# A decoder layer's trunk, run stage by stage over three token blocks instead of block by block, with Strassen's products added up in three PSUM banks

## The chip, the cores and the metric

The kernel runs on one core of a Trainium2 chip. The core has five engines with a queue of instructions each: TensorE (PE in the profile; its weight loads are PEld), VectorE (DVE), ScalarE (ACT), GpSimd (POOL) and SyncE (SP), which here only starts transfers. [...] The metric is device time in microseconds (us) from the start of the program to its end; lower is better.

## What is computed

One inference step of a decoder layer for 2048 prompt tokens and 32 sample tokens (8 requests of 4), all in float32, width 1024. First come the input projection, a gated linear recurrence on half of the heads and dilated window attention on the other half. The change touches none of that. It touches the trunk that follows, whose core in the reference is:

```python
mix = jnp.concatenate([o_a.astype(dt), o_b.reshape(bsz, t_len, B_WIDTH).astype(dt)], axis=-1)
h = x + mix @ w_o
hn = rmsnorm(h, norm_ffn_g)
u = hn @ w_gate
full = jnp.concatenate([conv_buf.astype(dt), u], axis=1)
c = conv_b
for j in range(CONV_W):
    c = c + conv_w[j] * full[:, j:j + t_len]
h = h + (jax.nn.silu(c) * (hn @ w_up)) @ w_down
new_conv = full[:, t_len:]
gate = jax.nn.sigmoid(rmsnorm(h, norm_ple_g) @ w_ple_gate)
h = h + gate * (p_emb.astype(dt) @ w_ple_proj)
```

w_gate and w_up are 1024 x 2816, w_down is 2816 x 1024, w_o and w_ple_gate are 1024 x 1024, w_ple_proj is 256 x 1024; the convolution runs over three neighbouring tokens of the same request. A final norm gives y.

## The kernel before

Features lie on partitions and tokens along the row. The trunk takes the tokens in three blocks: 704, 704 and 672 wide, the last of them 640 prompt tokens and the 32 sample tokens.

A float32 product is made from three matmuls (`mm3`, lines 131 to 134): an operand is split into a rounded part (ScalarE's copy) and the rest (a subtraction), and high by high, high by low and low by high are added up in PSUM. A weight is loaded 128 x 512 at a time, and `split` (lines 925 to 929) lets ScalarE round it (line 927) and VectorE and GpSimd by turns subtract (line 928).

`trunk_phase` (line 897) is one token block from start to end:

- **Out projection** (lines 968 to 1108): loads of the mix, 8 x 2 x 8 products of three matmuls, addition of x (line 1103). While it runs, the Strassen operands are made from h and the gains alone (`operands`, lines 989 to 1007), with subtractions on VectorE and GpSimd; the norm's factor per token (`rb`) is multiplied in later.
- **FFN** (lines 1163 to 1192): features two tiles of 128 at a time, eleven such pairs. Gate and up are one Strassen call each. `quarters` (line 1011) loads four weight quarters, GpSimd makes their four sums and differences, and all seven are split. `strassen` (line 1030) runs seven products of 12 matmuls over half a block of tokens, each into a bank of its own, and then puts them together: one copy on ScalarE (line 1042) and seven additions on VectorE (lines 1043 to 1049). `conv` (line 1111) multiplies by `rb` (lines 1115 and 1133) beside the convolution proper and copies the two border columns on VectorE (lines 1113 and 1120). The down projection of a pair (line 1157) is 16 output tiles of 6 matmuls, one behind another, each added into h by VectorE (line 1142); it runs one pair later, between gate and up.
- **Embedding stage** (lines 1195 to 1291): norm, `w_ple_gate`, sigmoid, `w_ple_proj`, final norm, output.

The norms' sums of squares go through small matmuls: columns (`rstd_cols`, line 105), a few small VectorE instructions (lines 91 to 96), and rows again (`bcast_rows`, line 120).

The phases of two blocks are stepped by turns (lines 1402 to 1413), so that the loads and the first out projection of block b+1 are written between the last embedding pieces of block b. h and all operands of a block stay in SBUF throughout. Products, downs and the rest share six banks, the norms have two.

The order of the instructions on each engine is not the order of the code: a planner simulates the program, and each engine takes the ready instruction that stands earliest in the code. On the chip the order is fixed, and an engine waits at an instruction whose inputs are late. All of the trunk's transfers are issued on SP's queue, except copies of the caches from DRAM to DRAM, which ScalarE's queue issues behind chosen rounding copies (`copy_after`).

## Time and profile before

| | |
|---|---|
| median of three runs | 3204.1 us (3198.14 to 3208.56) |
| the profiled execution's own time | 3206.86 us |
| its span, first to last instruction | 3204.7 us |
| busy in the span: TensorE, VectorE, GpSimd, ScalarE | 95%, 78%, 46%, 38% |
| mean granted clock of TensorE | 0.974 |
| traffic, mean | 408.89 MB, 128 GB/s |

Matmuls overlap each other in the trace, so TensorE's busy time hides short gaps; counts of matmuls per stretch of time tell more. A line number is that of the instruction's line in the kernel, often in a helper. A group's row gives line, engine, operation, output and inputs with their shapes, count, then busy us, mean ns of one, and the idle time of its engine before it with what ended it.

### The profile page before, as it was taken

To read this page: it belongs to the slowest core of one execution; us is meant where nothing else is said; L and a number is where in the kernel's file an instruction comes from. 1 tells how busy PE (TensorE), PEld (TensorE's weight loads), DVE (VectorE), ACT (ScalarE), POOL (GpSimd) and SP (SyncE) were. 2 spreads that over 40 slices of the span, in tenths; PEclk is the share of its full clock that TensorE was granted. 3 is DMA by queue.
4 is the path that set the end of the run, shared out by engine and by line. 5 is a ranking of instruction groups with operands and counts; after the bars stand their busy time and mean duration, and the time that the engine had idled before them with its cause. 6 is when DMAs were issued, how large, how long until landed. Compare 5 with 4: busy or idle time off the path is not lost.

```text
span 3204.7 us, 52298 instructions
## 1 busy us (share of the span) xinstructions
PE 3036.5 (95%) x19035; PEld 2795.5 (87%) x19035; DVE 2487.8 (78%) x4808; ACT 1226.7 (38%) x2441; POOL 1488.1 (46%) x1097
## 2 busy tenths in 40 slices
PE   8999999999889997899999999999999989999998
PEld 8988899977666666899999999999999988999998
DVE  6514588676788865888998758899998579999996
ACT  4112322221466653433334425333334244333343
POOL 1201122221454416656566458466564575655654
PEclk9999999999889998999999999999999999999999
DMA  5324333332456985343334242334433323433432
GB/s 181 105 102 145 93 113 115 121 126 82 118 135 191 266 278 162 105 130 113 119 126 140 80 136 68 129 126 136 134 117 105 99 94 128 136 124 106 130 109 79
DMA packets 241313, 408.89 MB, mean 128 GB/s; under 512 B 36832, under 2 KB 104544, under 8 KB 239264
## 3 DMA queue, kind: packets, MB, share of 16 engines
q1 hardware_dynamic: 237472, 338.57, 34.3%
q10 hardware_dynamic: 3584, 66.98, 6.2%
q8 instruction: 150, 2.46, 0.3%
q14 instruction: 107, 0.88, 0.1%
HBM read 347.52 MB, written 124.92 MB: 147 GB/s over the span
## 4 chain that ended last, share of the span: by engine, by line
PE 65%; DVE 24%; issue 4%; DMA 3%; POOL 2%; ACT 2%; ACTq 0%; SPq 0%; DVEq 0%; POOLq 0%
PE mm L132 14%; PE mm L133 13%; PE mm L134 13%; PE mm L297 2%; PE mm L298 2%; PE mm L299 2%; DVE w L1130 2%; DVE w L928 2%; DVE u L1115 2%; DVE w L1142 2%; PE acc L740 2%; PE lv L437 2%; DVE w L1131 2%; PE PT L728 2%; DVE w L1133 1%
## 5 line engine op out<-in xcount | busy, mean ns | idle before, releaser
L928 POOL TENSOR_TENSOR w<-raw,w 128x512 fp32r<-128x512 f32 x359 | 553.9, 1547 | 539.5 <-ACT w L927 537.2
L132 PE MATMUL mm<-w 128*128 128x352 f32 (+2 forms) x2070 | 681.2, 329 | 57.3 <-DVE w L1142 33.8
L927 ACT CAST w<-raw 128x512 fp32r<-128x512 f32 x718 | 433.5, 620 | 651.2 <-PE mm L134 524.2
L133 PE MATMUL mm<-w 128*128 128x352 f32 (+2 forms) x2070 | 667.7, 323 | 2.2 <-DVE w L1202 2.2
L134 PE MATMUL mm<-w 128*128 128x352 f32 (+2 forms) x2070 | 667.2, 322 | 0.0
L132 PE MATMUL mm<-x,w 128*128 128x352 f32 (+3 forms) x1686 | 547.1, 325 | 20.7 <-DVE w L1103 14.4
L133 PE MATMUL mm<-x,w 128*128 128x352 f32 (+3 forms) x1686 | 544.4, 323 | 2.5 <-DVE x L914 2.5
L134 PE MATMUL mm<-x,w 128*128 128x352 f32 (+3 forms) x1686 | 543.8, 323 | 0.0
L132 PEld LDWEIGHTS mm<-w 128*128 128x128 f32 x2070 | 393.0, 190 | 88.0 <-DVE w L1142 60.9
L928 DVE TENSOR_TENSOR w<-raw,w 128x512 fp32r<-128x512 f32 x359 | 392.6, 1095 | 46.4 <-ACT w L927 45.6
L133 PEld LDWEIGHTS mm<-w 128*128 128x128 f32 x2070 | 394.8, 191 | 3.1 <-DVE w L1202 3.1
L134 PEld LDWEIGHTS mm<-w 128*128 128x128 f32 x2070 | 393.5, 190 | 0.0
L132 PEld LDWEIGHTS mm<-x,w 128*128 128x128 f32 x1686 | 321.5, 191 | 22.8 <-issue 15.8
L133 PEld LDWEIGHTS mm<-x,w 128*128 128x128 f32 x1686 | 323.0, 192 | 3.3 <-DVE x L914 3.3
L134 PEld LDWEIGHTS mm<-x,w 128*128 128x128 f32 x1686 | 321.2, 191 | 0.1
L1142 DVE TENSOR_TENSOR w<-w,mm 128x352 f32<-128x352 f32 (+1 forms) x528 | 246.1, 503 | 6.5 <-PE mm L134 6.4
L138 POOL TENSOR_SCALAR wh<-wraw 128x512 fp32r<-128x512 f32 x96 | 72.1, 763 | 246.8 <-PE o L133 81.8
L721 ACT ACTIVATE P<-P,st 128x256 f32<-128x256 f32 (+3 forms) x256 | 134.5, 527 | 82.2 <-DVE st L720 79.6
L1058 POOL TENSOR_TENSOR w<-w 128x704 f32<-128x704 f32 (+2 forms) x63 | 121.6, 1930 | 83.3 <-ACT w L1057 78.5
L1016 POOL TENSOR_TENSOR raw<-raw 128x512 f32<-128x512 f32 x66 | 101.5, 1538 | 123.3 <-DMA raw<-in_w_up_dram 76.6
L914 DVE TENSOR_TENSOR w<-w 128x704 fp32r<-128x704 f32 (+1 forms) x84 | 139.5, 1667 | 5.1 <-ACT w L913 4.9
L297 PE MATMUL mm<-wh,xh 128*128 128x512 f32 x352 | 142.0, 405 | 0.0
(358 smaller groups left out, 6252.9 us busy)
## 6 DMA issues: line engine op xcount, KB each, us to landing
raw<-in_w_gate_dram SPq DMA_DIRECT2D x132, 256.0 KB
raw<-in_w_up_dram SPq DMA_DIRECT2D x132, 256.0 KB
raw<-in_w_down_dram SPq DMA_DIRECT2D x132, 256.0 KB
out_sk_dram<-in_cache_k_dram ACTq DMA_DIRECT2D x56, 584.0 KB
out_sv_dram<-in_cache_v_dram ACTq DMA_DIRECT2D x56, 584.0 KB
wraw<-in_w_in_dram SPq DMA_DIRECT2D x104, 256.0 KB
raw<-in_w_ple_gate_dram SPq DMA_DIRECT2D x64, 256.0 KB
raw<-in_w_o_dram SPq DMA_DIRECT2D x48, 256.0 KB
```

The costliest lines, as they stand in the source:

```text
L132: PE.matmul(ps, lhsT=wh, rhs=xh, start=first, stop=False)
L133: PE.matmul(ps, lhsT=wh, rhs=xl, start=False, stop=False)
L134: PE.matmul(ps, lhsT=wl, rhs=xh, start=False, stop=last)
L138: G.tensor_scalar(hi, x, 1.0, 1.0, op0=ALU.mult, op1=ALU.mult)
L297: PE.matmul(ps, lhsT=xh[k][:, js], rhs=wh, start=k == 0, stop=False)
L721: A.activation(pe, pe, AF.Exp, bias=mn, scale=-1.0, accum_out=st[:, bl.r, hh, 0:1])
L914: V.tensor_sub(lo, x, f32(hi))
L927: A.copy(w[:, 0], raw)
L928: next(subs).tensor_sub(w[:, 1], raw, f32(w[:, 0]))
L1016: G.tensor_add(s1, a21, a22)
L1058: eng.tensor_add(ssq[:, cs], ssq[:, cs], sq)
L1142: V.tensor_add(h[m][:, cs], h[m][:, cs], ps[:, :cn])
```

## The change

The trunk becomes three stages, each over all three blocks: out projection, FFN, embedding. Between them a block goes through DRAM: `h_d` holds h after the out projection, `hn_d` the same normed and scaled by the gains, `h2_d` h after the FFN.

- **Out projection**: after its eight tiles a block's norm is made and applied to h by eight VectorE instructions, and h and the normed h are stored. All roundings are ScalarE's.
- **Operands** (`factors`) are read back from `hn_d` in three parts (products 1, 2, 3; then 5, 6; then 7, 4). All their subtractions are VectorE's; the second half of the 3-4 operand has its sign turned.
- **Strassen**: products 1, 6, 7, 4 add up in one bank, 5 and 3 in a second, 2 has a third. ScalarE copies the running sum after 1, 6 and 7, and copies one result; three VectorE additions make the other three. Results go straight into the convolution's input, so `conv` has no multiplication by the norm's factor. The border columns are copied by ScalarE.
- **Downs** stand in a list; a fixed number of them is taken after each product (`gate`, `up`). 24 of a block's last downs are left for the start of the next block, or for the start of the embedding stage.
- **Weights**: `split` subtracts on VectorE alone; GpSimd keeps the four sums per call. The weight order follows the new order of use.
- **Pools**: all eight banks in one pool; 48 block-wide tiles in place of 16 and 32, 9 split weights in place of 11, 8 raw tiles in place of 9, and 6 half-block tiles for copied sums.

Counts of matmuls and their widths stay. The last embedding block ends as before.

```diff
-USE = (1, 2, 6, 7, 5, 3, 4)
+USE = (1, 5, 6, 2, 7, 4, 3)
...
+    h_d, hn_d, h2_d = [dram.tile([128, NK, NTOK], F32, name=n) for n in ("h_d", "hn_d", "h2_d")]
...
-            next(subs).tensor_sub(w[:, 1], raw, f32(w[:, 0]))
+            V.tensor_sub(w[:, 1], raw, f32(w[:, 0]))
...
+        def out_block(b):
...
+                for ps, c0, cn in dense_all(w, chunks, mh, ml, first[m] if m < 2 else None):
+                    V.tensor_add(hm[:, c0:c0 + cn], ps[:, :cn], xr[:, c0:c0 + cn])
+                SP.dma_start(h_d[:, m, t0:t0 + T], hm)
+                sum_sq(m, hm, ssq, T)
+                h.append(hm)
+                yield
+            rb = rstd(ssq, T)
+            for m in range(NK):
+                V.scalar_tensor_tensor(h[m], h[m], gains[:, 1, m:m + 1], rb, op0=ALU.mult, op1=ALU.mult)
+                SP.dma_start(hn_d[:, m, t0:t0 + T], h[m])
...
+        def factors(b, X):
...
+            for i in range(4):
+                xa, xb = x(i, one), x(i + 4)
+                b11 = wide(T, F32R)
+                A.copy(b11[:, one], xa[:, one])
+                V.tensor_sub(b11[:, two], xa[:, one], f32(b11[:, one]))
+                X[1][i] = b11[:, one], b11[:, two]
+                hi, lo = both(xb)
...
+            for i in range(4):
+                xa, xb = x(i), x(i + 4, two)
+                t12 = wide(T)
+                V.tensor_sub(t12[:, one], xa[:, two], xa[:, one])
+                V.tensor_sub(t12[:, two], xb[:, two], t12[:, one])
+                hi, lo = both(t12)
...
+                A.copy(t2[i], t12[:, two])
...
+            for i in range(4):
+                xa, xb = x(i, two), x(i + 4)
+                t34 = wide(T)
+                V.tensor_sub(t34[:, one], xb[:, two], xa[:, two])
+                V.tensor_sub(t34[:, two], xb[:, one], t2[i])
+                hi, lo = both(t34)
...
+            pa, pb, pc = acc_tile(), acc_tile(), acc_tile()
+            product(pa, 1)
+            s1 = copied()
+            product(pb, 5)
+            product(pa, 6, False)
+            s2 = copied()
+            product(pc, 2)
+            put(0, 0, lambda o, v: V.tensor_add(o, v(pc), v(s1)))
+            product(pa, 7, False)
+            s3 = copied()
+            put(1, 1, lambda o, v: V.tensor_add(o, v(pb), v(s3)))
+            product(pa, 4, False)
+            put(1, 0, lambda o, v: A.copy(o, v(pa)))
+            product(pb, 3, False)
+            put(0, 1, lambda o, v: V.tensor_add(o, v(pb), v(s2)))
...
+            next(make)
+            down(8)
...
+                if f == 0:
+                    gate = {1: 4, 5: 0, 6: 4, 2: 8}
...
+                    gate = dict(zip(USE, (0, 1, 1, 1, 1, 0, 0) if last else (0, 0, 1, 1, 2, 1, 0)))
...
+                up = dict(zip(USE, (0, 1, 1, 1, 1, 0, 0) if last else (1, 2, 2, 2, 2, 1, 1)))
...
+        for stage in (out_block, ffn_block, embed_block):
+            for b in range(len(TRUNK)):
+                for _ in stage(b):
+                    pass
+            down(100)
...
+        trunk(cst, pool("tr", 8), pool("te", 3), pool("ts", 1), pool("tw", 48), pool("th", 6), pool("tp", 9),
+              pool("tm", 8, space=PSUM))
```

More of the change, by code (lines that the diff above doesn't have):

```diff
@@ L969, in trunk_phase, with sum_sq @@
[L969 to L976 removed]
+        def sum_sq(m, h, ssq, T, cs=None, eng=V):
+            cs = cs or slice(0, T)
+            if m == 0:
+                A.activation(ssq[:, cs], h[:, cs], AF.Square)
+            else:
+                sq = wide(T)[:, cs]
+                A.activation(sq, h[:, cs], AF.Square)
+                eng.tensor_add(ssq[:, cs], ssq[:, cs], sq)
```

541 lines of the change are left out of this document (241 added, 300 removed).

## The prediction

> **What bounds the kernel now.** I read the page first, then the busy time by stretches of the trunk, then who TensorE waited for there, and last the groups of one long FFN stretch.
>
> ```profile
> span 3204.7 us, 52298 instructions
> PE 3036.5 (95%) x19035; PEld 2795.5 (87%) x19035; DVE 2487.8 (78%) x4808; ACT 1226.7 (38%) x2441; POOL 1488.1 (46%) x1097
> PE 65%; DVE 24%; issue 4%; DMA 3%; POOL 2%; ACT 2%; ACTq 0%; SPq 0%; DVEq 0%; POOLq 0%
> ```
>
> TensorE is the frame of everything, and VectorE holds a quarter of the chain that ended last. The trunk starts at about 1231 us. Below are its stretches; the columns are the stretch, its length, busy time and (number of instructions) of TensorE, weight loads, VectorE, ScalarE and GpSimd, granted TensorE clock, DMA share and GB/s.
>
> ```profile
> 1231.00:1250.00 19.00, 16.93 (x91) 16.93 (x92) 10.12 (x8) 7.17 (x13) 10.99 (x7) 0.81 0.64 194
> 1250.00:1395.00 145.00, 134.50 (x820) 132.78 (x819) 122.82 (x160) 65.76 (x103) 97.32 (x64) 0.96 0.32 107
> 1395.00:1800.00 405.00, 394.47 (x2420) 387.17 (x2419) 365.06 (x506) 156.20 (x243) 234.76 (x148) 1.00 0.38 122
> 1800.00:2040.00 240.00, 222.01 (x1332) 218.50 (x1331) 179.20 (x248) 94.89 (x152) 147.37 (x96) 0.95 0.33 110
> 2040.00:2450.00 410.00, 402.03 (x2476) 394.58 (x2476) 368.19 (x516) 156.85 (x246) 231.90 (x150) 1.00 0.38 122
> 2450.00:2700.00 250.00, 226.82 (x1402) 222.07 (x1401) 191.14 (x287) 99.68 (x162) 153.86 (x100) 0.96 0.33 108
> 2700.00:3055.00 355.00, 338.85 (x2112) 328.03 (x2111) 327.73 (x515) 133.03 (x222) 213.09 (x138) 0.99 0.37 119
> 2120.00:2150.00 30.00, 30.00 (x190) 30.00 (x189) 25.73 (x30) 11.85 (x19) 23.22 (x16) 1.00 0.53 168
> 3046.00:3074.00 28.00, 28.00 (x184) 28.00 (x183) 24.93 (x40) 12.87 (x23) 17.39 (x12) 1.00 0.39 130
> ```
>
> Matmuls overlap, so busy time flatters; I count instead. The last two rows have no gap: 30/190 = 0.158 us per matmul of 352 columns (blocks 0 and 1) and 28/184 = 0.152 us for 336 (block 2). What a stretch took beyond its count times this floor is lost. FFN stretches: 405 - 2420 x 0.158 = 22.6, 410 - 2476 x 0.158 = 18.8, 355 - 2112 x 0.152 = 34.0; together **75.4 us**. Around and between blocks: 4.6, 15.4, 29.5, and 32.7 (at 0.155, both widths occur); together **82 us**, where the clock of 0.95 to 0.96 has its part. By the code an FFN pair of feature tiles (two Strassen calls of 84 matmuls, 16 down tiles of 6) is 264 matmuls, so the three FFN stretches hold 9.2, 9.4 and 8.0 pairs, 26.6 in all, and a pair takes 44.2, 43.7 and 44.4 us where its floor is 41.7, 41.7 and 40.1. A pair with fewer columns takes as long: that is no TensorE pace. VectorE's share of the three is 90%, 90% and 92%.
>
> ```profile
> PE mm L132 <- DVE w L1142: 33.8, 45, 1.8
> PE mm L132 <- DVE w L1103: 15.6, 5, 4.8
> PE mm L132 <- ACT w L1042: 14.0, 3, 5.2
> PE ms L120 <- DVE rs_v L111: 10.3, 4, 4.8
> ```
>
> These are TensorE's own waits in the trunk (sum, times, longest). The first is in the pairs: a bank of a down product that VectorE has not yet added into h (line 1142). The others are single holes of up to 5.2 us where a block starts (line 1103: out projection; 1042: first Strassen; 120: the norm's rows).
>
> **The change, part by part.** The matmuls stay: seven products of 12 per Strassen call, as many tiles elsewhere. So the floor stays and the sum is about the 157 us lost. VectorE first, from the first FFN stretch, grouped:
>
> ```profile
> L928 POOL TENSOR_TENSOR w<-raw,w 128x512 fp32r<-128x512 f32 x80 | 125.7, 1576 | 125.4 <-ACT w L927 125.3
> L928 DVE TENSOR_TENSOR w<-raw,w 128x512 fp32r<-128x512 f32 x80 | 89.5, 1118 | 6.1 <-ACT w L927 6.1
> L1142 DVE TENSOR_TENSOR w<-w,mm 128x352 f32<-128x352 f32 x158 | 74.4, 508 | 2.2 <-PE mm L134 2.2
> L914 DVE TENSOR_TENSOR w<-w 128x704 fp32r<-128x704 f32 x18 | 32.3, 1796 | 0.0
> L1115 DVE TENSOR_TENSOR u<-w 128x704 f32<-128x704 f32 x18 | 25.6, 1422 | 0.3
> L1133 DVE TENSOR_TENSOR w<-w 128x704 f32<-128x704 f32 x18 | 19.3, 1073 | 0.0
> L1129 ACT ACTIVATE w<-u,taps 128x704 f32<-128x704 f32 x18 | 17.6, 977 | 43.7 <-DVE u L1115 43.7
> L1120 DVE COPY halo<-u 128x2 f32<-128x2 f32 x18 | 11.6, 645 | 0.0
> L1049 DVE TENSOR_TENSOR w<-w,mm 128x352 f32<-128x352 f32 x18 | 9.3, 514 | 2.4 <-PE mm L134 2.4
> L1042 ACT COPY w<-mm 128x352 f32<-128x352 f32 x17 | 7.7, 452 | 12.6 <-PE mm L134 10.5 <-issue 2.1
> L1113 DVE COPY u<-halo 128x2 f32<-128x2 f32 x15 | 3.4, 227 | 0.0
> L928 POOL TENSOR_TENSOR w<-raw,w x80: 1280/1588/2087, 1395.3 to 1793.5; 128x512 fp32r<-128x512 f32 x80
> L928 DVE TENSOR_TENSOR w<-raw,w x80: 674/748/1823, 1397.3 to 1792.4; 128x512 fp32r<-128x512 f32 x80
> ```
>
> (The last two rows are the view of line 928 alone: min/median/max ns.) Today a pair costs VectorE 365.06/9.2 = 39.7 us. Running sums in PSUM leave three VectorE additions of seven per Strassen call: 8 x 0.514 = 4.1 us less. Operands normed beforehand drop lines 1115 and 1133: 2 x 1.422 + 2 x 1.073 = 5.0 less. The halo copies move to ScalarE: 2 x 0.645 + 2 x 0.227 = 1.7 less. All 18 weight subtractions are VectorE's instead of nine: 9 x 1.118 = 10.1 more. That is 39.0, hardly anything, if durations stay. They should not: the same subtraction takes 0.674 at best and 1.118 on average, and GpSimd, busy 234.76/9.2 = 25.5 us per pair, gives up 9 x 1.576 = 14.2 and keeps 44%. The excess on 18 subtractions, 18 x 0.444 = 8.0 us, cut to 44%, is 3.5: so 34.5 us per pair, 83% of TensorE's 41.7. The bounds are 31.0 (no excess left) and 39.0 (all of it). The row nearest to 83% is the gapless 2120 to 2150, where VectorE was busy 86%.
>
> ScalarE gets three more copies out of PSUM per Strassen call: 156.20/9.2 = 17.0 us plus 6 x 0.452 and some small ones, about 20.5 of 41.7. The downs, until now a run of 16 behind one another, are dealt out one or two behind each product, and the banks become one pool of eight of which Strassen takes three; a late addition then delays one bank of five, not the next matmul. What replaces it is a new wait: products 6, 7 and 4 go on adding in a bank that ScalarE has just copied. In a gate call product 5 stands between (12 matmuls, 1.9 us against a copy of 0.452), then 24 matmuls, then two downs (1.9 us); in an up call more. Queued behind a late one are all later products. No row shows this wait; its bounds are zero and one ScalarE operation ahead in the queue, 0.977, on each of six products: 5.9 us per pair. I take 0.6 us lost per pair for the two wide blocks, near the gapless row, and 1.5 in block 2, where VectorE starts from 92% and the sample rows' small instructions stay: 18.6 x 0.6 + 8 x 1.5 = **23 us** instead of 75, between 0 and 26.6 x 3 = 80.
>
> Now the stage order. All three blocks of the out projection run first. Each transfer's size, and a stretch that shows what the queues can do:
>
> ```profile
> u<-mix_d SPq DMA_DIRECT2D x16, 352.0 KB
> raw<-in_w_o_dram SPq DMA_DIRECT2D x48, 256.0 KB
> 1170.00:1250.00 80.00, 56.84 (x433) 39.60 (x432) 42.05 (x109) 28.14 (x76) 25.10 (x19) 0.79 0.82 252
> ```
>
> A block moves mix, x, h and normed h (8 x 352 KB each) and 16 weight halves: 15.7 MB, in 384 x 0.158 = 60.7 us, 259 GB/s, where 252 took a share of 0.82. It fits, with 16% to spare on a queue in order, and a store that waits for its norm stands before later loads on SP. I take 5 us per block, 15; bounds 0, and 53 at 200 GB/s. The first block's own start stays (4.6).
>
> The first FFN block has no downs to cover its operands. Per token block these are twelve full and twenty half subtractions: at 1.796 (line 914) down to 1.073 (line 1133) for a full one and 0.514 for a half, 23 to 32 us of VectorE, against 84 matmuls (13.3 us) of the first gate call; a part can be made while the last out block runs, as far as tiles are free (28 operand tiles, some 28 in use there, 48 in all). I take 12 us, between 0 and 25. The two other FFN blocks start under 24 downs held back for them: 312 matmuls, 49 us, against VectorE's 23 to 32 plus 24 x 0.508 plus 18 subtractions of 0.674 to 1.118, so 47 to 64: short by 0 to 15, I take 8 each, 16. Into and between embed blocks 5 (0 to 10): their loads are of rows written long before. Sum 4.6 + 15 + 12 + 16 + 5 = **53 us** instead of 82. The last block's end is the old one.
>
> [...]
>
> Gain: (75 - 23) + (82 - 53) = 81 us. The profiled execution took 3206.9 for a span of 3204.7; the median of the runs shown is 3204.1. 3206.9 - 81 = 3126, by the median 3123: I say **3125**.
>
> **The rivals.**
> *All covered* (0.12): pairs at their floor (5 us lost in all), boundaries 25: 75 + 82 - 30 = 127 gained, 3078. For it: the gapless rows; against it: the 47 to 64 us of VectorE in 49.
> *VectorE stays the pace* (0.14): subtractions stay at 1.118, 39.0 us per pair, and operands come on top; pairs lose what they lose now, boundaries gain 14: 3190. For it: 39.0 is 94% of 41.7. Against it: 14 us of GpSimd gone. [...]
> *Out stage at the queue's pace* (0.10): at 200 GB/s, 53 lost in place of 15: 3163. Against it: 252 was reached.
> *The wait moves to the shared bank* (0.14), slower. Products 6, 7, 4 of both calls wait for ScalarE's copy, behind an operation that itself waits for VectorE, since ScalarE works in order. Loss 0.8 each, 4.8 us per pair instead of 0.87, over 33 pairs: 130 more, 3255. It is slower than the old kernel from (0.87 + 81/33)/6 = 0.55 us per product on.
>
> ```profile
> ACT w L1129 <- DVE u L1115: 43.7, 18, 5.3
> ACT w L1132 <- DVE w L1131: 38.6, 17, 4.8
> ```
>
> For it: ScalarE stood 2.4 and 2.3 us per convolution behind VectorE, up to 5.3. Against it: today's copy (1042) held TensorE three times only.
>
> **How the numbers follow.** The forecast has 0.50, its own range 3095 to 3165. 0.3% is 9.6 us, about what a measurement of this kernel can tell from no change. Faster: 0.50, 0.12, 0.10 and 0.08 of VectorE's 0.14, so 0.80; the other 0.06 is the same; slower 0.14. The range 3080 to 3205 leaves out the shared bank and half of *all covered*.
>
> **What would show it.** Pairs of 42 to 43 us, and the same count per stretch; VectorE near 83% there, its weight subtraction near 0.85 us instead of 1.118; no TensorE wait on the down additions. TensorE waiting for ScalarE's copies by over 3 us per pair, or a pair of 44 us with VectorE over 90%, would make me wrong; so would an out stage over 240 us for its 1152 matmuls or a hole over 25 us ahead of the first gate product.

## The result and the profile after

The changed kernel takes **3285.2 us** (median of four runs, 3281.9 to 3287.4) where the kernel before takes 3206.3 on the same chip (3198.1 to 3211.8). The ratio is 1.0247, with a 95% interval from 1.0222 to 1.0272. The forecast of 3125 us, and of faster, was wrong by 160 us. The profiled execution took 3285.15 us.

From the page of the changed kernel: span, busy time, the chain that ended last by engine, and the group of the weight subtraction.

```profile
span 3283.3 us, 52038 instructions
...
PE 3053.0 (93%) x19035; PEld 2820.1 (86%) x19035; DVE 2249.6 (69%) x4679; ACT 1304.7 (40%) x2825; POOL 821.3 (25%) x646
...
PE 82%; DVE 9%; DMA 4%; ACT 2%; issue 2%; SPq 1%; POOL 0%; DVEq 0%; ACTq 0%; POOLq 0%
...
L914 DVE TENSOR_TENSOR w<-raw,w 128x512 fp32r<-128x512 f32 x718 | 548.0, 774 | 182.4 <-ACT w L913 178.5
```

VectorE did leave the chain: 9% instead of 24%. All 718 weight subtractions are now VectorE's and take 0.774 us in the mean; the half that it had before took 1.118 in the first FFN stretch. Yet the span is longer. The stretches tell where; the columns are those of the same view in the prediction. The rows are three out blocks, the start of FFN block 0, its pairs, a boundary, the pairs of block 1, a boundary, the pairs of block 2, and three embedding blocks.

```profile
1231.00:1300.00 69.00, 64.88 (x384) 64.14 (x384) 34.77 (x53) 22.24 (x34) 0.00 (x0) 0.94 0.64 213
1300.00:1376.00 76.00, 67.11 (x414) 66.14 (x414) 39.86 (x70) 22.19 (x34) 0.00 (x0) 0.96 0.62 209
1376.00:1452.00 76.00, 67.40 (x416) 66.34 (x415) 43.84 (x70) 22.40 (x37) 11.17 (x7) 0.91 0.52 176
1452.00:1545.00 93.00, 57.94 (x252) 50.30 (x253) 56.10 (x88) 35.13 (x64) 11.67 (x8) 0.69 0.49 173
1545.00:1950.00 405.00, 405.00 (x2536) 405.00 (x2536) 305.33 (x461) 178.19 (x346) 133.18 (x77) 1.00 0.38 129
1950.00:2045.00 95.00, 75.34 (x404) 69.69 (x403) 68.13 (x107) 39.01 (x72) 18.59 (x12) 0.87 0.60 203
2045.00:2450.00 405.00, 405.00 (x2537) 405.00 (x2536) 308.25 (x465) 180.28 (x353) 131.79 (x76) 1.00 0.38 127
2450.00:2540.00 90.00, 67.87 (x355) 62.46 (x354) 63.60 (x101) 36.88 (x74) 18.46 (x12) 0.81 0.58 199
2540.00:2950.00 410.00, 410.00 (x2676) 410.00 (x2675) 341.20 (x556) 196.08 (x416) 112.72 (x74) 1.00 0.41 140
2950.00:3055.00 105.00, 84.60 (x508) 82.31 (x506) 54.28 (x104) 37.55 (x62) 17.31 (x10) 0.92 0.28 96
3055.00:3170.00 115.00, 93.41 (x527) 90.82 (x527) 61.98 (x110) 41.39 (x68) 20.49 (x11) 0.86 0.29 99
3170.00:3284.00 114.00, 88.02 (x525) 84.16 (x525) 72.42 (x150) 42.68 (x78) 23.02 (x20) 0.87 0.29 103
```

Counted as in the prediction (time beyond count times floor):

| stretch | lost, us | forecast |
|---|---|---|
| pairs of the three FFN blocks | 4.3 + 4.2 + 3.2 = 11.7 | 23 |
| out stage | 8.3 + 10.6 + 12.8 = 31.7 | 19.6 with the first start |
| start of FFN block 0 | 53.2 | 12 |
| two FFN boundaries | 31.2 + 35.0 = 66.2 | 16 |
| embedding blocks 0 and 1 | 24.7 + 31.7 = 56.4 | 5 |

The pairs have no gap at all: a stretch of 405 us holds TensorE busy for 405. Everything that lies between stages went wrong: 207.5 us instead of 53, and the granted clock is 0.69 to 0.96 there against 1.00 in the pairs. The last embedding block, which the forecast left as it was, is worse too. This row is the kernel before, its last 114 us:

```profile
3091.00:3205.00 114.00, 99.16 (x647) 97.12 (x645) 80.75 (x153) 47.20 (x84) 57.36 (x45) 0.95 0.24 80
```

It holds 647 matmuls where the last 114 us after hold 525; 122 x 0.152 = 18.5 us. The sum closes against the forecast: 154.5 more between the stages, 18.5 at the end, 11.3 less in the pairs, 161.7 us against a miss of 160.2.

TensorE's own waits in the trunk after the change (sum, times, longest):

```profile
PE mm L136 <- ACT w L1021: 36.9, 13, 4.6
PE mm L123 <- DVE rs_v L114: 23.0, 8, 4.1
PE mm L136 <- ACT w L1034: 17.4, 8, 5.7
PE mm L137 <- DVE w L1236: 16.5, 5, 6.2
PE mm L108 <- POOL w L961: 11.3, 2, 5.7
PE mm L137 <- DVE w L1035: 10.2, 5, 6.1
...
PE mm L136 <- ACT s L1089: 3.0, 6, 0.6
```

Lines 1021, 1034 and 1035 are roundings and a subtraction of the Strassen operands, 114 and 961 the norms, 1236 the operands of the embedding stage. The copy of a running sum (1089), the wait that was feared most, cost 3.0 us in all. There is no single large hole. At the start of FFN block 0 TensorE has 16 waits, 35.1 us together and 6.1 us at the longest, and behind the longer ones its matmuls start 0.29 us apart (1481.39 to 1485.21) instead of 0.16. The granted clock of this stretch is 0.69. Over the rows from 1231 to 3170 outside the pairs the waits come to 139 us of the 207.5; the rest has no wait to name, and the slow matmuls are part of it.

The norm's columns and rows are now a hole that the next block doesn't fill. The end of out block 0, a timeline:

```profile
1300.36 1.68 PE L108 MATMUL mm<-ones,w 128*128 128x2 f32 x12 [2.37 <-DVE w L961]
...
1304.56 2.93 PE L123 MATMUL mm<-c_ident,rs_y 128*128 128x128 f32 x12 [2.53 <-DVE rs_v L114]
...
1306.68 0.58 ACT L132 COPY w<-mm 128x512 f32<-128x512 f32 x1 [7.30 <-PE mm L123]
1307.16 0.78 ACT L982 CAST w<-u 128x704 fp32r<-128x704 f32 x1
...
1307.99 1.63 PE L136 MATMUL mm<-w 128*128 128x352 f32 x8 [0.50 <-ACT w L982]
```

ScalarE stood idle for 7.30 us and then copied the norm's rows; only behind that came the first rounding of out block 1 (line 982), though its input was on the chip: three of block 1's eight rows of the mix had been loaded early, the last of them issued at 1248.83. The next block's first matmul ran at 1307.99. Last the groups of the first FFN boundary, 1952 to 2012 us:

```profile
L1022 DVE TENSOR_TENSOR w<-w 128x704 fp32r<-128x704 f32 x12 | 11.8, 982 | 4.4 <-ACT w L1021 4.3
...
L1021 ACT CAST w<-w 128x704 fp32r<-128x704 f32 x12 | 9.4, 780 | 20.3 <-DVE w L1045 9.5 <-DVE w L1056 8.4 <-DMA w<-hn_d 2.3
...
L1034 ACT CAST w<-w 128x352 fp32r<-128x352 f32 x4 | 1.9, 482 | 7.0 <-DMA w<-hn_d 7.0
```

The whole chain of a block's operands (load, subtraction, rounding, subtraction) lies inside this window, with ScalarE waiting for loads and for VectorE in between. Part of it is also a rush on the transfers: from 2005 to 2015 us, in the same boundary, the DMA share is 0.96 at 335 GB/s, and from 1460 to 1470, at the start of FFN block 0, it is 1.00 at 345 GB/s. No run made these loads smaller, so what the rate itself costs there is open.

### The profile page after: what moved, and what is told of

Read it like the earlier page. It is cut to its first block, busy times and chain, and to the rows that moved or that the text cites. A ratio compares the mean times of both kernels' runs of the same rounds, so it can differ in the third digit from the quotient of the medians.

```text
span 3283.3 us, 52038 instructions
## 1 busy us (share of the span) xinstructions
PE 3053.0 (93%) x19035; PEld 2820.1 (86%) x19035; DVE 2249.6 (69%) x4679; ACT 1304.7 (40%) x2825; POOL 821.3 (25%) x646
## 4 chain that ended last, share of the span: by engine, by line
PE 82%; DVE 9%; DMA 4%; ACT 2%; issue 2%; SPq 1%; POOL 0%; DVEq 0%; ACTq 0%; POOLq 0%
PE mm L137 19%; PE mm L136 18%; PE mm L138 18%; PE mm L301 2%; PE mm L302 2%; PE mm L303 2%; PE acc L744 2%; PE PT L732 2%; DMA w<-hn_d 2%; PE lv L441 1%; DMA w<-h_d 1%; PE S L719 1%; PE lv L301 1%; PE lv L303 1%; PE lv L302 1%
## 5 line engine op out<-in xcount | busy, mean ns | idle before, releaser
L137 PE MATMUL mm<-w 128*128 128x352 f32 (+3 forms) x3768 | 1224.3, 326 | 37.9 <-DVE w L1236 16.5
L136 PE MATMUL mm<-w 128*128 128x352 f32 (+3 forms) x3768 | 1187.2, 326 | 73.4 <-ACT w L1021 36.9
L138 PE MATMUL mm<-w 128*128 128x352 f32 (+3 forms) x3768 | 1211.6, 324 | 0.0
L136 PEld LDWEIGHTS mm<-w 128*128 128x128 f32 x3768 | 714.5, 192 | 89.0 <-ACT w L1021 42.1
L137 PEld LDWEIGHTS mm<-w 128*128 128x128 f32 x3768 | 722.2, 192 | 49.3 <-DVE w L1236 20.6
L138 PEld LDWEIGHTS mm<-w 128*128 128x128 f32 x3768 | 721.0, 192 | 0.1
L914 DVE TENSOR_TENSOR w<-raw,w 128x512 fp32r<-128x512 f32 x718 | 548.0, 774 | 182.4 <-ACT w L913 178.5
L1067 POOL TENSOR_TENSOR raw<-raw 128x512 f32<-128x512 f32 x66 | 116.5, 1765 | 697.1 <-DVE w L914 285.9
L1075 POOL TENSOR_TENSOR raw<-raw 128x512 f32<-128x512 f32 x66 | 86.5, 1310 | 524.9 <-DVE w L914 524.9
L1089 ACT COPY s<-mm 128x352 f32<-128x352 f32 (+1 forms) x198 | 88.1, 447 | 262.4 <-PE mm L138 260.0
L303 PE MATMUL mm<-wh,xl 128*128 128x512 f32 x352 | 140.9, 401 | 0.0
L302 PE MATMUL mm<-wl,xh 128*128 128x512 f32 x352 | 140.4, 400 | 0.0
L136 PE MATMUL mm<-xh,wh 128*128 128x384 f32 (+2 forms) x384 | 125.1, 330 | 5.9 <-ACT xh L199 5.1
L1072 POOL TENSOR_TENSOR raw<-raw 128x512 f32<-128x512 f32 x66 | 127.9, 1938 | 2.6
L138 PE MATMUL mm<-xh,wl 128*128 128x384 f32 (+2 forms) x384 | 125.2, 329 | 0.6 <-DVE wl L224 0.5
L137 PE MATMUL mm<-xl,wh 128*128 128x384 f32 (+2 forms) x384 | 124.5, 327 | 0.6 <-DVE xl L200 0.6
```

What stands on the lines that cost most here:

```text
L136: PE.matmul(ps, lhsT=wh, rhs=xh, start=first, stop=False, skip_group_check=read)
L137: PE.matmul(ps, lhsT=wh, rhs=xl, start=False, stop=False, skip_group_check=read)
L138: PE.matmul(ps, lhsT=wl, rhs=xh, start=False, stop=last, skip_group_check=read)
L302: PE.matmul(ps, lhsT=xh[k][:, js], rhs=wl, start=False, stop=False)
L303: PE.matmul(ps, lhsT=xl[k][:, js], rhs=wh, start=False, stop=k == NK - 1)
L914: V.tensor_sub(w[:, 1], raw, f32(w[:, 0]))
```

## The experiments

Theories at the start: **A**, what stands later in the code starts later, because the planner and the pools hand out tiles and turns in the order of the code, and a stage over three blocks writes block b+1 wholly behind block b; **B**, the trip of h through DRAM (the wait for what was stored, and the traffic); **C**, the order of SP's queue. For the pairs: is it VectorE's sum, GpSimd's company, or the running sums? Diffs are against the changed kernel (experiments 1 to 5, 7 to 9, 15, 17, 18) or the kernel before (the others). A time without a range or an interval is that of a single execution; the four of the changed kernel lie within 5.5 us, so a difference of 5 us shows nothing.

**1. Out stage written by turns.** The generators of the out blocks are stepped so that the loads and roundings of block b+1 stand among the last tiles of block b.

```
-        for stage in (out_block, ffn_block, embed_block):
+        outs = [out_block(b) for b in range(len(TRUNK))]
+        go(outs[0], NK + 1)
+        for a, b in zip(outs, outs[1:]):
+            go(a, 2)
+            for k in range(4):
+                go(a, 1); go(b, 2)
...
+        for stage in (ffn_block, embed_block):
```

> Changed kernel; in the out stage alone the loads of block b+1 and its first four dense groups stand in the code by turns with the last tiles of block b. Same instructions and transfers. Counted as in the prediction, the out stage (1231 to 1452 us, 1214 matmuls) lost 31.7 us, the start of the first FFN block 53, the next two 31 and 35, the embedding stage 25, 32 and 35. Theory A (a pool hands out its tiles in the order of the code, so a block's operands wait for the last tile of the block before, the row of its norm): the out stage loses about 12, the whole takes 20 us less, 3265, and the later stretches stay. Theory B (the trip through DRAM, its latency and traffic) and theory C (a store that waits stands in front of loads on SP): same transfers, so no change, 3285.

Measured: 3266.1, 19 less. The same 1224 instructions on TensorE, first in the changed kernel, then here:

```profile
1232.00:1458.00 226.00, 202.32 (x1224) 199.26 (x1224) 119.76 (x204) 67.06 (x107) 11.17 (x7) 0.92 0.58 196
```

```profile
1229.00:1440.00 211.00, 197.53 (x1224) 195.48 (x1223) 115.53 (x206) 67.58 (x107) 10.11 (x7) 0.95 0.63 212
```

Order alone gives 15 us of it at the same traffic; A holds for the out stage.

**2. First part of the operands early.** `next(makes[b + 1])` behind product 6 of the last up call, instead of in the next block.

> Changed kernel; the first part of the next FFN block's operands stands in the code behind product 6 of the last up call instead of behind the last pair's products. Same instructions and transfers. Theory A: the boundaries of FFN blocks 1 and 2, which lose 31 and 35 us, lose about 12 each, 3242; the first FFN start stays at 53. Theory B: unchanged, 3285. Theory C: unchanged or up to 8 us per boundary less, since the loads then stand ahead of the stores, 3270 to 3285.

Measured: 3277.0, 8 less where 43 were expected. Only the first third of the operands was moved; the other two parts still stand at the first gate call. At the first boundary TensorE's waits for the first third (lines 1034 and 1035, 7.0 us) are gone and those for the other two (line 1021) nearly stay, 9.2 us instead of 10.0, although their loads came earlier (the last was issued by 1993.8 instead of 2005.4). And a new wait has come up: 6.6 us instead of 0.8 for the rounding of the last pair's gated operand (line 1223 here, 1217 in the changed kernel). It waited for VectorE, which worked without a gap from 1947.6 to 1957.4 us.

**3. No stores of h2.**

```
-                if f == NF - 2 and c0:
-                    SP.dma_start(h2_d[:, m, t0:t0 + T], h[m])
...
-                SP.dma_start(hm, h2_d[:, m, t0:t0 + T])
+                SP.dma_start(hm, h_d[:, m, t0:t0 + T])
```

> Changed kernel without the 24 stores of h behind the FFN; the embedding stage reads h as it was before the FFN, so the FFN's addition is missing in y. Theory C: in the trace SP stood 7.8 us before one such store at the start of FFN block 1 with operand loads behind it; the two boundaries and the start of the embedding stage lose 8 us less each, 3261. Theory A: 3285, unchanged. Theory B: unchanged at the FFN boundaries, the start of the embedding stage a few us less.

Measured: 3271.4, 14 less. This kernel's y lacks the FFN's addition. In the trace of the changed kernel SP issued operand loads up to 1954.6, then nothing until a store at 1962.4 and more operand loads from 1964.1: C is real. Of the 14 us some 9 lie at the two FFN boundaries; the embedding stage gained a little too, but it also read older rows here.

**4. Operands from x instead of the normed h.**

```
-                SP.dma_start(t[:, cs], hn_d[:, i, t0:t0 + T][:, cs])
+                SP.dma_start(t[:, cs], I["xT"][128 * i:128 * i + 128, t0:t0 + T][:, cs])
```

> Changed kernel; the Strassen operands are read from the input x in place of the normed h, in the same sizes, so they do not depend on anything that the kernel writes to DRAM (u and all that follows is computed from x). Theory B: the three FFN starts lose about 15 us each instead of 53, 31 and 35, 3210. Theories A and C: the loads are issued where they were, unchanged within 5 us, 3285.

Measured: 3288.0, no change. With operand loads that depend on no store the time is the same, so that part of B falls; the traffic was the same in this run.

**5. The old split in the changed kernel.**

```
-            V.tensor_sub(w[:, 1], raw, f32(w[:, 0]))
+            next(subs).tensor_sub(w[:, 1], raw, f32(w[:, 0]))
```

> Changed kernel, but the weights are subtracted by VectorE and GpSimd by turns again, as before the change. What made the pairs gapless? If it is VectorE's relief from additions and norm products (4.1 + 5.0 + 1.7 us per pair), the pairs stay near 42.2 us: nine subtractions of 0.77 leave VectorE, nearly as much comes back as contention, total 3280 to 3295. If it is GpSimd's relief, VectorE slows as before, the pairs go back to about 44 us and the total to 3335.

Measured: 3297.7, 12 more. A stretch of pairs:

```profile
1550.00:1950.00 400.00, 400.00 (x2495) 400.00 (x2494) 278.15 (x373) 179.59 (x343) 248.56 (x161) 1.00 0.39 127
```

GpSimd is busier than in the kernel before (62% against 234.76/405 = 58%), and TensorE still has no gap. In the changed kernel the pairs don't need GpSimd's relief; the time is just above the 3280 to 3295 expected for that case.

**6. The new split in the kernel before**, the reverse line alone:

```
-            next(subs).tensor_sub(w[:, 1], raw, f32(w[:, 0]))
+            V.tensor_sub(w[:, 1], raw, f32(w[:, 0]))
```

> Kernel before, with all weight subtractions on VectorE, nothing else. If VectorE's sum per pair sets the pace there: 39.7 us plus nine subtractions, less contention, is 43 to 45 us, pairs of 46 to 48 us, 3260. If contention with GpSimd is what costs, VectorE falls under 40 us per pair and the kernel gains, 3180.

Measured: **3169.5**, 37 less than the kernel before on the same chip (3206.9), though VectorE got more instructions:

```profile
1395.00:1800.00 405.00, 401.32 (x2478) 394.91 (x2478) 378.03 (x595) 161.29 (x251) 113.97 (x73) 1.00 0.38 123
```

VectorE is at 93% instead of 90%, and 58 more matmuls run in the same 405 us. So 90% of VectorE was not by itself what held the pairs. TensorE's waits for the down additions (line 1142) fell from 33.8 us to 12.2.

**14. The new split and the halo copies on ScalarE, in the kernel before.**

```
-            V.tensor_copy(u[:, 0:2], cst["halo"][:, f])
+            A.copy(u[:, 0:2], cst["halo"][:, f])
...
-            V.tensor_copy(cst["halo"][:, f], u[:, npr:npr + 2])
+            A.copy(cst["halo"][:, f], u[:, npr:npr + 2])
```

> The kernel before with the weight subtractions on VectorE and the halo copies on ScalarE, no running sums. VectorE per pair 40.3 - 1.7 = 38.6 us. If VectorE's sum still holds the pairs: some 8 us under the subtractions alone (3169.5), 3162. If contention was all: 3167 to 3172. It also shows whether ScalarE's halo copies, which stand before the next gated operand on ScalarE, cost anything: then above 3175.

Measured: **3139.4** (3132.4 to 3142.4; before 3209.5), ratio 0.9779, interval 0.9762 to 0.9796. This is the fastest kernel of the study, under both kernels. Two stretches:

```profile
1395.00:1800.00 405.00, 402.67 (x2517) 400.04 (x2515) 376.40 (x578) 166.00 (x287) 115.95 (x71) 1.00 0.38 125
2040.00:2400.00 360.00, 358.30 (x2233) 355.96 (x2232) 339.17 (x513) 143.55 (x253) 97.82 (x61) 1.00 0.40 132
```

405 - 2517 x 0.158 = 7.3 and 360 - 2233 x 0.158 = 7.2 us are lost, with VectorE at 93 and 94%. The weight subtraction now takes 0.873 us in the mean of the first stretch. VectorE's other instructions became shorter, too. The clearest is the subtraction of the gated operand, here alone (min/median/max ns) in three kernels: the kernel before, this one, and the changed kernel, where it is line 1218.

```profile
L914 DVE TENSOR_TENSOR w<-w x18: 879/1977/1984, 1429.6 to 1772.1; 128x704 fp32r<-128x704 f32 x18
```

```profile
L914 DVE TENSOR_TENSOR w<-w x18: 875/877/1774, 1426.3 to 1756.2; 128x704 fp32r<-128x704 f32 x18
```

```profile
L1218 DVE TENSOR_TENSOR w<-w x18: 879/1978/1985, 1580.4 to 1919.3; 128x704 fp32r<-128x704 f32 x18
```

It has two durations and hardly any between. In the kernel before 15 of the 18 overlap in time with an operation of GpSimd and take 1.975 us or more; the three that don't take 0.887 or less. In experiment 14 one of 18 overlaps, and one takes 1.774 us where the mean of all is 0.927. In the changed kernel 16 of 18 do and take 1.968 us or more, though GpSimd makes only the sums there; the two that don't take 0.879 and 0.892. So in these two traces the time of this instruction goes with whether GpSimd is at work in that moment, not with which work it does.

The step from 3169.5 (one run) to 3139.4 is larger than the 8 us expected of two small copies. Some 6 us of it are in this first stretch, where 6 lost 405 - 2478 x 0.158 = 13.5; why it is so much is open.

**10, 11, 12. The running sums alone in the kernel before.** Ten has the new split, eleven also the halo copies, twelve the old split. `strassen` becomes

```
+            pa, pb, pc = [acc_tile()[:, :H] for _ in range(3)]
+            prod(pa, 1)
+            A.copy(c11, pa)
+            prod(pb, 5)
+            prod(pa, 6, False)
+            A.copy(c12, pa)
+            prod(pc, 2)
+            V.tensor_add(c11, pc, c11)
...
```

> The kernel before with the pair's part of the change alone: old stage order, norm after the products as before; Strassen's products share three banks with running sums copied out by ScalarE, and the weight subtractions all on VectorE. Counted at 0.158 and 0.152 us per matmul, the long FFN stretches of the run with the subtractions alone moved lost 405 - 2478 x 0.158 = 13.5, 410 - 2509 x 0.158 = 13.6 and 355 - 2213 x 0.152 = 18.6, 46 us, against about 12 in the whole change. Theory P (the pair's relief is worth the same in the old stage order, and only the stage order costs): 46 falls to about 12, so 3169.5 - 34 = 3135. Rival: the runs of 16 down products and the sums through the old path keep the waits, 3160 to 3170. Rival S (shared banks cost in the old order, where no down lies between the products): slower than 3175.

> As the running sums alone, and the halo copies moved from VectorE to ScalarE as in the change: 2 x 0.645 + 2 x 0.227 = 1.7 us less of VectorE per pair. If VectorE still sets the pace of the pairs: some 10 us less than the running sums alone. If the pairs are already at TensorE's pace: the same within 4 us.

> The kernel before with the running sums, but the old split of the weight subtractions in turns over VectorE and GpSimd. If the running sums (4.1 us less of VectorE per pair, and banks that come free sooner) suffice by themselves: as the running sums with all subtractions on VectorE, about 3135. If what holds the pairs is the contention between GpSimd's subtractions and VectorE: the gain of the moved subtractions (37 us) is missing, 3170 to 3180.

Measured: 3276.1 (ratio to before 1.0222, 1.0192 to 1.0252), 3266.1 (1.0182, 1.0150 to 1.0213) and 3288.2. All three expectations missed: with the sums the old kernel is slower than without, by 107 us from experiment 6 to 10 and 127 from 14 to 11. Their traces name one wait that the kernel before hardly has (0.4 us): TensorE for the rounding of the gated operand (line 913), 82.3 us in 24 holes in experiment 10.

**13. The whole pair part in the kernel before**: sums, split, halo copies, and the downs dealt out in the change's numbers.

```
+                deal(many[i])
...
+                cgs = strassen(wg, many=(0, 1, 1, 1, 1, 0, 0) if end else (0, 0, 1, 1, 2, 1, 0))
```

> The kernel before with the whole pair part of the change and none of its stage order or early norm: subtractions on VectorE, running sums in three banks, halo copies on ScalarE, and the 16 down products of a pair dealt out behind the products of the next pair in the change's numbers (the banks stay six and two). The running sums without the dealt order cost 107 us against the same kernel without them; their trace shows one hole of 3.4 us per pair (82.3 us over 24) where the first down product stands right behind the pair's last product and waits for its own gated operand. Theory P2 (the sums need the dealt order, and with it the pairs run without holes in any stage order): FFN loss about 12 instead of 46, so near 3135, and the change's loss is its stage order alone. Rival S2 (sums in shared banks are slow by themselves): above 3230. Rival between: the pairs run but the block ends stretch, since the last pair's downs are dealt as well: 3160 to 3200.

Measured: 3284.8 (1.0241, 1.0225 to 1.0256). Dealing didn't cure it. TensorE's wait in the trunk, and one of the holes in a timeline:

```profile
PE mm L132 <- ACT w L913: 131.6, 33, 8.2
```

```profile
1569.01 0.32 PE L134 MATMUL mm<-x,w 128*128 128x352 f32 x1
...
1571.28 0.88 DVE L1233 TENSOR_TENSOR w<-w 128x704 f32<-128x704 f32 x1
...
1572.19 0.78 ACT L913 CAST w<-w 128x704 fp32r<-128x704 f32 x1 [2.15 <-DVE w L1233]
...
1573.03 0.72 PE L132 MATMUL mm<-w 128*128 128x352 f32 x2 [3.70 <-ACT w L913]
1573.55 0.49 PE L133 MATMUL mm<-w 128*128 128x352 f32 x1
1573.84 0.49 PE L134 MATMUL mm<-w 128*128 128x352 f32 x1
...
1576.76 0.48 PE L132 MATMUL mm<-w 128*128 128x352 f32 x2
```

The pair's last product ends, VectorE multiplies gate by up (1233), ScalarE rounds the product (913), and TensorE waits for that. The row of two matmuls at 1573.03 is a lone one and the first of a product: behind it follow the eleven others of the next pair's first product, which needs nothing of the gated operand. The lone one is the first matmul of a down. The planner put it there, and none of the twelve started ahead of it: TensorE waited 3.70 us.

**16. The same with the downs queued behind the product that they follow in the code.** It adds an order on TensorE and no wait.

```
+                with tc.issue_after(end.ins):
+                    deal(many[i])
```

> The pair part alone with one addition: each down product is queued on TensorE behind the Strassen product that it follows in the code (an order on TensorE, no wait). In the trace of the pair part alone a single down matmul, which needs only the gated operand's rounded half, stood right behind the pair's last product and ahead of the next pair's first product, waited 3.9 us for ScalarE's cast, and the next 12 matmuls ran at half pace: 131.6 us of waits in 33 holes, with the slow matmuls behind them some 180 us. Theory O (the planner's place for that one matmul is all that made the sums slow): the holes go, pairs without loss as in the change, near 3110 and under the split and halo copies alone (3139). Rival (product 1 itself is late, its bank or its weights, and the down only stood ahead of it): the holes stay, named by a bank or a weight, above 3230.

Measured: **3155.8** (before 3212.5), ratio 0.9834, 0.9811 to 0.9857; 129 us less than experiment 13, from the downs' place in TensorE's queue. The same 300 us, experiment 13 and then 16:

```profile
1500.00:1800.00 300.00, 279.48 (x1690) 277.75 (x1689) 227.94 (x339) 121.84 (x230) 73.79 (x45) 0.97 0.36 119
```

```profile
1500.00:1800.00 300.00, 296.59 (x1852) 294.78 (x1851) 239.73 (x376) 131.99 (x245) 76.53 (x54) 1.00 0.37 125
```

162 more matmuls, and the wait for line 913 is gone. So theory O holds; the time of 3110 was missed, since 52.0 us of waits on the first copied sum came up, the longest 11.7 us at the start of a block's second pair. The sums bring the old kernel nothing over experiment 14 (3139.4), but in order they cost little. And this run prices the rest of the change, that is the stage order with its early norm, its trips through DRAM and its pools: the same pair part with the old stages is 129 us faster than the changed kernel (3285.2 - 3155.8, on two chips).

**7. All stages by turns**: out, first operand part and embedding blocks written as in 1 and 2.

> Changed kernel with the code order of the first two experiments together and the embedding stage's next block by turns with the last tiles of the block before. Same instructions and transfers. Theory A: out stage -19 and FFN boundaries -8 as measured singly; the embedding stage, which loses 13 at its start and 39 and 38 at its two changes of block, keeps the 13 and loses about 15 at each change: 3211. Theories B and C: the embedding stage as it is, 3258.

Measured: 3228.3, 57 less than the changed kernel. By equal counts of matmuls some 15 us of it lie in the out stage, 15 at the two FFN boundaries and 27 in the embedding stage. The start of FFN block 0 stayed as it was.

**8. As 7, with the 72 stores on GpSimd's queue and the operands of block 0 begun in the last out block.**

```
-                SP.dma_start(h_d[:, m, t0:t0 + T], hm)
+                G.dma_start(h_d[:, m, t0:t0 + T], hm)
```

> As the run before, and the first part of FFN block 0's operands stands within the last out block, four of the first embedding block's loads within the last up call, and the 72 stores of h, normed h and h2 are issued on GpSimd's queue. Theory C (a waiting store holds SP's loads): FFN boundaries lose about 12 instead of 28 and 32, the first FFN start about 25 instead of 46, 3155. Without C, with A alone: first FFN start about 30, 3195.

Measured: 3222.0, 6 less than in 7; 3155 and 3195 were expected. But the start of FFN block 0 did gain. The same 252 matmuls, first in experiment 7, then here:

```profile
1436.30:1525.70 89.40, 58.04 (x252) 50.63 (x253) 54.79 (x75) 35.08 (x64) 11.52 (x8) 0.70 0.50 175
```

```profile
1435.00:1511.50 76.50, 53.85 (x252) 49.03 (x253) 48.21 (x67) 30.36 (x56) 15.85 (x16) 0.78 0.46 160
```

That is 12.9 us. TensorE's waits for the first third of the operands (lines 1035 and 1036), 11.4 us in experiment 7, are gone from this stretch; the waits for the other two thirds, which were not moved, are there still (19.8 us). Other stretches lost part of the gain again; the pairs of block 2 took 417 us instead of 410. No store stands on SP now, and this is SP's timeline at the first FFN boundary:

```profile
1942.67 0.89 SPq L908 DMA_DIRECT2D raw<-in_w_gate_dram  x2
1943.65 1.81 SPq L1028 DMA_DIRECT2D w<-hn_d  x4
1954.31 0.90 SPq L908 DMA_DIRECT2D raw<-in_w_gate_dram  x2
1955.26 0.90 SPq L1028 DMA_DIRECT2D w<-hn_d  x2
```

Operand loads still stop for 9 us (1945.5 to 1954.3) ahead of a weight load. The next runs asked whether that load, or a tile, is what they wait for.

**9, 17. The operand loads on GpSimd's queue (changed kernel) and on ScalarE's (kernel of 7).**

```
-                SP.dma_start(t[:, cs], hn_d[:, i, t0:t0 + T][:, cs])
+                G.dma_start(t[:, cs], hn_d[:, i, t0:t0 + T][:, cs])
```

> The changed kernel with one edit: the loads of the normed operands (line 1027) are issued by GpSimd's queue and no longer by SP's. Theory C (the rest of the lost boundary time is the order of SP's queue: these loads stand behind weight loads that wait for a free tile and behind a store that waits for its sum): first FFN start 49 to about 35, the two FFN boundaries 30 and 35 to about 15 each, together some 50 us less, 3235. Rival A2 (the loads wait for free tiles, whichever queue they stand in): unchanged, 3280 to 3290. A third way: GpSimd, which also adds the weight quarters, is held up behind a load that waits for a tile, and it becomes slower, above 3295.

> The kernel with the code order by turns in all stages (3228), with the loads of the normed operands issued by ScalarE's queue instead of SP's, where no weight load stands ahead of them. GpSimd's queue was no test of that, since GpSimd waits for weight tiles as SP does. Theory C (these loads stand behind weight loads that wait for a free raw tile): first FFN start 48 to about 25, FFN boundaries 27 and 25 to about 12, 3178 to 3195. Rival (the operands' own chain of casts and subtractions, 12 x 2.5 us beside the downs' additions, is what the products wait for): within 8 us of 3228.

Measured: 3302.7 (17 more) and 3247.7 (19 more). Neither queue helps, so nothing is left of C beyond the 14 us of experiment 3. Why both runs are slower was not shown.

**15. 44 wide tiles instead of 48.**

> The changed kernel with 44 instead of 48 of the wide tiles that operands, h and sums share. Theory T (what is left of the boundary time after the code order is a shortage of free tiles when the next block's operands are loaded): out stage, FFN start and FFN boundaries all grow, together by 30 us or more, above 3315; the pairs by nothing. Rival (the loads wait for their turn in the queue, not for tiles): within 6 us of 3285.

Measured: 3289.1, no change. The last four of the 48 tiles are not the limit; more than 48 were not tried.

**18. Embedding blocks between the FFN blocks.**

```
+        for b in range(len(TRUNK)):
+            for _ in ffn_block(b):
+                pass
...
+            go(embs[b], NK + 1 + 1 + 5)
+            next(makes[b + 1])
+            go(embs[b], 100)
```

> The kernel with the code order by turns (3228), and the stages of the FFN and the embedding no longer apart: FFN block 0, embedding 0, FFN block 1, embedding 1, FFN block 2, embedding 2; the first third of the next block's operands is made behind the sixth embedding row. No operation is added or removed. Theory V (cover: at an FFN boundary only 24 down products, about 23 us, stand between the last product that holds the old operands and the first that needs the new ones, while the kernel before had an embedding and an out projection there): the waits ahead of the first gate products of blocks 1 and 2, 27 and 25 us, fall to 12 or less each, since some 70 us of embedding products lie there; the embedding's own starts stay 14 to 25 each; in all 3190 to 3215. Rival (the operands' chain is slow wherever it lies, by queues or by its place in the code): 25 us or more remain at each, and the total is 3228 or above.

Measured: 3275.6 (two runs, 3271.1 and 3280.1), 47 more than in 7, where 13 to 38 less were expected. TensorE at the start of FFN block 1:

```profile
2058.10 0.60 PE L136 MATMUL mm<-w 128*128 128x352 f32 x1
...
2068.16 0.95 PE L136 MATMUL mm<-w 128*128 128x352 f32 x2 [7.69 <-ACT w L1022]
...
2096.62 0.66 PE L136 MATMUL mm<-w 128*128 128x352 f32 x1 [4.89 <-ACT w L1022]
```

The first product starts at 2058.10 without a wait: its operands are the third that the code makes early. Product 5 then waits 7.69 us for the second third, whose code stands at the gate call, and later ones for the last third, now without a down to cover them. So the 70 us of embedding products were no use to what stood behind them in the code. That is A again; whether enough cover would do once all three thirds are written early was not tried.

## Why the prediction was wrong

**The pairs: right in kind, too careful.** The three VectorE additions of seven and the 34.5 us of VectorE per pair became 305.33/9.61 = 31.8 us (76% of 41.7), near the lower bound of 31.0; the weight subtraction took 0.774 us instead of the 0.85 forecast. Pairs took 405/9.61 = 42.2 us, as forecast, and lost 11.7 us instead of 23.

**Reading VectorE's 90% as the pairs' pace was wrong, behind a right number.** Experiments 6 and 14 raise VectorE to 93 and 94% and lose less than the kernel before at 90%. A part of its busy time goes with GpSimd's work beside it: in the kernel before the subtraction of line 914 took 1.975 to 1.984 us with a GpSimd operation beside it and 0.879 to 0.887 without. It isn't all: experiment 5 has GpSimd at 62% and no gap, so the change's sums, downs and early norm make enough room by themselves; which of them does was not told apart.

**"The wait moves to the shared bank" (0.14), the rival on the slow side: wrong place.** It gave 3255 and so the sign, by luck: the copies of the running sums held TensorE for 3.0 us in the whole trunk.

**"All covered", "VectorE stays the pace", "Out stage at the queue's pace"** all fall, the last one not by its rate: the out stage ran at 176 to 213 GB/s, close to the rival's 200 and well under the 259 that the forecast needed. But experiment 1 took 15 us out of the 31.7 lost there at 212 GB/s without touching a transfer, so half of it was order.

**The failed step is the boundaries, 53 us forecast and 207.5 measured.** The single term with the largest miss is "I take 12 us, between 0 and 25" for the start of the first FFN block: 53.2. The step rested on "a part can be made while the last out block runs, as far as tiles are free". The code wrote the part later, and so it came later: the rounding of the mix stood behind the norm's rows (1306.68 and 1307.16), the operands behind the last out block. Experiment 8 writes one third of them early, and this start gives back 12.9 us.

The two FFN boundaries were reckoned as 47 to 64 us of VectorE under 49 us of matmuls. Only 24 x 6 x 0.158 = 22.8 us of these are downs; the other 168 matmuls are the gate and up products, of which the first must wait for the operands they were to cover. And the reckoning was by throughput, where the work is a chain of load, subtraction, rounding, subtraction, in which ScalarE stood 20.3 us.

"Into and between embed blocks 5" assumed that rows written long before load early; 56.4 us were lost. Of TensorE's waits there, 15.3 us are for the stage's operands (1235, 1236) and 22.7 us for the norms (961, 114), which the forecast did not count between blocks. And "The last block's end is the old one" missed 18.5 us.

How much has been shown: order of the code in the out stage 15 to 19 us (1), at the start of FFN block 0 13 (8, in which the stores were moved too), in all stages 57 (7); SP's store 14 (3); not the wait for DRAM (4), not the queue of the loads (9, 17), not the last four tiles (15). Some 100 us of the 154 stay without a run that gives them back. That two thirds of the operands still stood at the gate call in every run is the likeliest cause of the FFN part; it is argued from 2, 8 and 18, not shown. Writing a third early also brings another wait, the one for the gated operand, 12.9 us in experiment 7. And the cause was not told apart from the 28 operand tiles that the old block holds until its last products, nor from the full DMA engines in those moments (share 0.96 and 1.00).

**Slow matmuls behind holes have no term of their own in the forecast.** In experiment 13 a hole of 3.9 us (1569.01 to 1573.03, less one matmul) is followed by matmuls 0.29 us apart for 3.7 us (1573.03 to 1576.76) instead of 0.16, 1.6 us lost. At the start of FFN block 0 alone, 53.2 - 35.1 = 18 us were lost beside the waits, at a granted clock of 0.69.

**The signs of "What would show it" didn't catch the miss.** Pairs took 42.2 us, the out stage 221 us (under 240), TensorE hardly waited for the copies (3.0 us), and no hole of over 25 us stood ahead of the first gate product: the longest wait in that stretch was 6.1 us. The sign named the right place, but the loss came as many short holes. Time lost per stretch, which the prediction had counted for the kernel before, would have been the better sign.

## What to carry over

When a phase order is turned into a stage order, count what TensorE has to do between the last use of the old operands and the first use of the new, and check in the code that the next block's loads and roundings are written ahead of the previous block's end; most work that could run early doesn't if the code puts it late. A sign that names one long hole misses a loss made of many short ones: add up the lost time of a stretch. A busy share is no bound by itself: in experiment 6 VectorE went from 90% to 93% with 89 instructions more in 405 us, 58 more matmuls ran in them, and GpSimd beside it was busy for 113.97 us instead of 234.76. Try each part of a change alone: one line of this one, with two copies moved, was worth 70 us, and the whole cost 79.

## What was not expected of the hardware

Nine weight subtractions per pair moved from GpSimd to the busier VectorE made the kernel before 37 us faster (experiment 6), with the subtraction on VectorE going from 1.118 to 0.873 us (experiment 14). The 704-wide subtraction of the gated operand on VectorE took 0.879 to 0.887 us in the kernel before where GpSimd was not at work beside it (3 of 18), and 1.975 to 1.984 where it was (15 of 18). And one matmul per pair at the wrong place in TensorE's queue, waiting 131.6/33 = 4.0 us with matmuls 0.29 us apart behind it instead of 0.16 (1573.03 to 1576.76), is the main part of 129 us over 33 pairs (13 against 16, where all downs were put in order).
